# Two product sums in two PSUM banks per FFN unit, and two slot pools of six in a two-layer decoder trunk

## The chip, the cores and the metric

The kernel runs on one core of one Trainium2 chip. The metric is the device time of one execution in microseconds (us); the value for a kernel is the median over several executions. A profile is one more execution, recorded instruction by instruction. Engines: PE multiplies matrices (PEld is its weight load), DVE, ACT and POOL work on vectors, SP issues the transfers (DMA). PE writes its results to PSUM, eight banks of 512 numbers of 32 bits per partition; DVE and ACT read them there.

## The reference, cut to what matters

Two layers; each has two SwiGLU sub-layers (FFN), a token mixing and a per-layer embedding gate. All is computed in 32 bits, for 512 tokens of width 1024 and an FFN width of 2816.

```python
def swiglu(x, w_in, w_out):
    gate, up = jnp.split(x @ w_in, 2, axis=-1)
    return (jax.nn.silu(gate) * up) @ w_out

for l in range(DEPTH):                       # DEPTH = 2
    x = x + 0.5 * rms_norm(swiglu(rms_norm(x, ln_ffn1_pre[l]), w_ffn1_in[l], w_ffn1_out[l]), ln_ffn1_post[l])
    mix = token_mixing(rms_norm(x, ln_mix_pre[l]), ...)
    x = x + rms_norm(mix, ln_mix_post[l])
    x = x + 0.5 * rms_norm(swiglu(rms_norm(x, ln_ffn2_pre[l]), w_ffn2_in[l], w_ffn2_out[l]), ln_ffn2_post[l])
    gate = jax.nn.sigmoid(rms_norm(x, ln_ple_pre[l]) @ w_ple_gate[l])
    x = x + rms_norm(gate * (p[l] @ w_ple_proj[l]), ln_ple_post[l])
```

## The kernel before

**Precision.** A 32-bit operand is split into a high part (ACT, line 139) and a remainder, the low part (DVE, or POOL where a call says so, line 140). A product is three matmuls: high by high (L167), high by low (L168), low by high (L169); the third needs the low part of the weights.

**FFN-in** (function `ffn`) goes over 22 *units* m of 128 columns of gate and the 128 columns of up beside them. A unit is a 2 by 2 product of blocks done with seven products instead of eight; product n multiplies one combination of weight blocks with one combination of activation blocks (`right[n]`), in 4 slices of 3 matmuls of 256 columns, so 84 matmuls a unit. Products 1, 2, 3 and 5 have plain activations on the right (`xh`, `xl`; rows "p<-xh,w" and "p<-xl,w"), 4, 6 and 7 have sums of them (`tx`, rows "p<-tx,w"). On the left stand weights: `w12` (w1 for the first four units), `w75`, `w63` and `w4`; `ws` are the sums of blocks from which w75 and w63 are split (DVE lines 355, 357, 358). The split weights w12, w75 and w63 share NW = 3 buffers in the pool `wsp`, so the next unit's w12 is split once product 2 of this unit has read its own.

After the products DVE and ACT add the seven results up (lines 351 and 367 to 382) to `gate` (called a) and `up` (b), ACT applies Silu, DVE multiplies into `h`. A unit uses four of the eight PSUM banks: pa for products 1 and 2, pc for 6 and 3, pb for 7 and 5, pd for 4, each product in its own half of a bank.

At the **head** of FFN-in the four token blocks are turned (`turn`, PE transposes); for the last two of them the sums for tx are formed (lines 238 to 242), one of them (line 242) on POOL, which also splits three of the sums and the low parts of the first weights w1.

**FFN-out** (`ffn_out`) takes eleven blocks b of h in two column halves: seven as S blocks with seven-product sums, whose weights are loaded into `ws_r` (line 440) and read by PE as they are, four as plain P blocks, whose split h (`hq`) is kept for the second half. `us` holds evacuated sums at the end of a half.

**Slots.** Tiles of 8 KB (raw weights `wr`, `ws_r`, `hq`, h, tx, `xr`, `us`, split weights of some blocks) come from one pool of NS = 12; a load waits on SP's queue until a slot is free, and everything behind it in the queue waits as well.

**The order** on each engine is not the order of the code: the framework's scheduler sets it with its own timing model and fixes it at build time. Each engine then works strictly in that order.

Of the kernel before, what the change touches and what calls it, by code (L numbers as in the profile page):

```python
# [9 lines left out]
F32 = mybir.dt.float32  # L10
F32R = mybir.dt.float32r
# [6 lines left out]
S = 512  # L18
# [5 lines left out]
NS, NW = 12, 3  # L24
G = 4
# [47 lines left out]
class Trunk:  # L73
# [91 lines left out]
    def mm3(self, out, a, b, first, last):  # L165
        mm = self.nc.tensor.matmul
        mm(out, a[0], b[0], start=first, stop=False)  # L167
        mm(out, a[0], b[1], start=False, stop=False)  # L168
        mm(out, a[1], b[0], start=False, stop=last)  # L169
# [40 lines left out]
    def turn(self, t, xn, ffn):  # L210
# [31 lines left out]
        g_.tensor_tensor(t4, t4, t2, ALU.add)  # L242
# [19 lines left out]
    def out_proj(self, nb, part, blocks, gain, scale, after, tail):  # L262

        half0 = []
        for h in range(2):
# [13 lines left out]
            if h and tail == nb:  # L279
                raws = [q[:, j] for q in [self.slot([2, 1024], "wor") for _ in range(nb // 2)] for j in range(2)]  # L280
# [43 lines left out]
    def ffn(self, l, w, after):  # L324
# [15 lines left out]
        def product(n, q, out):  # L340
            for k in range(4):
                self.mm3(out, [a[:, k * 128:(k + 1) * 128] for a in q], [b[:, k] for b in right[n]], k == 0, k == 3)

        def left(m):
            r = self.ffn_raw[m] if m < G else self.ffn_load(l, w, [m])[0]
            return r, self.mm_tile("p12"), self.tmp.tile([128, S], F32, tag="tb0", name="gate", bufs=4)

        def gate(m, pa, a, q):
            product(1, self.cut(q, lo), pa[:, L])
            product(2, self.cut(q, hi), pa[:, H])  # L350
            a_.activation(a[:, (H, L)[m % 2]], pa[:, L], AF.Copy)

        def unit(m, r, pa, a):
# [11 lines left out]
            P, Q = (L, H) if m % 2 else (H, L)  # L365
            product(6, self.cut(sy, lo), pc[:, L])
            v_.tensor_tensor(a[:, Q], pc[:, L], a[:, P], ALU.add)
            product(7, self.cut(sx, lo), pb[:, P])
            product(5, self.cut(sx, hi), pb[:, Q])
            v_.tensor_tensor(b.rearrange("p (i t) -> p i t", i=2), pb.rearrange("p (i t) -> p i t", i=2),  # L370
                             a[:, None, Q].to_broadcast([128, 2, 256]), ALU.add)
            v_.tensor_tensor(a[:, P], pa[:, H], a[:, P], ALU.add)
            product(3, self.cut(sy, hi), pc[:, H])
            v_.tensor_tensor(a[:, Q], pc[:, H], b[:, Q], ALU.add)  # L374
            v_.tensor_tensor(b[:, Q], pb[:, Q], b[:, P], ALU.add)
            a_.activation(a, a, AF.Silu)  # L376
            product(4, u2, pd[:, L])
            v_.tensor_tensor(b[:, P], b[:, P], pd[:, L], ALU.subtract)
            if m % 4 == 0:
                hs.append(self.slot([8, 256], "h"))  # L380
# [18 lines left out]
    def ffn_out(self, hs, blocks, gain, scale, after):  # L399
# [50 lines left out]
        for h in range(2):  # L450
# [35 lines left out]
            us = self.slot([4, 512], "us")  # L486
# [1027 lines left out]
```

## Time and profile before

| | |
|---|---|
| median of 3 runs | 2292.49 us (2291.95 to 2295.7) |
| profiled execution | 2293.78 us, its span 2292.1 us |
| PE busy | 2154.4 us, 94% of the span |
| DVE busy | 1735.3 us, 76% |
| ACT busy | 1006.8 us, 44% |
| POOL busy | 330.7 us, 14% |
| FFN-in, first to last product | 17.44 to 289.99, 710.58 to 976.07, 1154.79 to 1426.45, 1845.73 to 2109.00 us |

The execution's own time is 1.7 us longer than its span, which runs from the first to the last instruction. A matmul's row lasts 0.28 us while the next starts 0.12 us after it: matmuls overlap, so a time per matmul is read from how many start in a stretch, not from a row's length. In rows of instructions, "[2.12 <-ACT w L139]" means that the engine stood idle for 2.12 us before this instruction until ACT's instruction of line 139 on tile w released it. PEclk is the clock that PE was granted, 1.00 being full speed.

### The profile page before, as it was taken

What the parts mean: (1) busy time and instruction counts of PE and PEld (TensorE: products, weight loads), DVE (VectorE), ACT (ScalarE), POOL (GpSimd) and SP (SyncE); (2) the same over time, 40 slices, a digit from 0 to 9 for tenths busy, and PEclk for the clock granted to TensorE, in tenths of its full rate; (3) what the DMA queues carried; (4) which work ended last, traced back from release to release, by engine and by line L of the source; (5) the groups of instructions that cost most, each with busy time, mean ns of one, the idle gap of its engine ahead of it and who ended that gap; (6) DMA issues with size and microseconds to landing.
All of it is one profiled execution on the core that took longest, in us unless ns stands there. A gap on an engine that the chain in (4) does not pass through costs nothing.

```text
span 2292.1 us, 39759 instructions
## 1 busy us (share of the span) xinstructions
PE 2154.4 (94%) x16256; PEld 1991.3 (87%) x16256; DVE 1735.3 (76%) x2886; ACT 1006.8 (44%) x1653; POOL 330.7 (14%) x424
## 2 busy tenths in 40 slices
PE   5999999999988999999979999999999989999998
PEld 5998999888767998999879899998887789899996
DVE  8988886555768888886688888775557698888774
ACT  4343433446545443433554344344464454344343
POOL 4000001132234000002330000111322330000111
PEclk9999999999999999999989999999999999999999
DMA  5222123322032222123322122243220322122232
GB/s 211 93 74 75 65 83 129 124 74 56 20 146 94 93 74 74 65 83 129 138 111 86 62 84 70 78 142 121 61 60 12 147 111 93 56 92 74 90 115 73
DMA packets 67495, 208.61 MB, mean 91 GB/s; under 512 B 15728, under 2 KB 16752, under 8 KB 67312
## 3 DMA queue, kind: packets, MB, share of 16 engines
q1 hardware_dynamic: 67312, 206.07, 25.5%
q8 instruction: 127, 2.08, 0.4%
q14 instruction: 56, 0.46, 0.1%
HBM read 199.23 MB, written 6.82 MB: 90 GB/s over the span
## 4 chain that ended last, share of the span: by engine, by line
PE 74%; DVE 12%; ACT 5%; DMA 3%; issue 3%; POOL 1%; SPq 0%; ACTq 0%; DVEq 0%; POOLq 0%
PE y L463 14%; PE p L169 12%; PE p L167 12%; PE p L168 12%; DVE w L140 2%; PE pkrv L169 1%; PE pkrv L168 1%; PE pkrv L167 1%; DVE xn L207 1%; PE y L169 1%; PE y L168 1%; PE y L167 1%; ACT w L139 1%; PE pgt L167 1%; PE pgt L168 1%
## 5 line engine op out<-in xcount | busy, mean ns | idle before, releaser
L167 PE MATMUL p<-xh,w 128*128 128x256 f32 x1408 | 415.9, 296 | 50.7 <-ACT w L139 46.3
L169 PE MATMUL p<-xh,w 128*128 128x256 f32 x1408 | 415.5, 295 | 9.8 <-POOL w L140 6.4
L168 PE MATMUL p<-xl,w 128*128 128x256 f32 x1408 | 411.6, 293 | 0.2 <-DVE xl L140 0.2
L167 PEld LDWEIGHTS p<-xh,w 128*128 128x128 f32 x1408 | 283.4, 202 | 57.0 <-ACT w L139 50.4
L167 PE MATMUL p<-tx,w 128*128 128x256 f32 x1056 | 301.3, 289 | 15.5 <-ACT tx L139 11.7
L168 PE MATMUL p<-tx,w 128*128 128x256 f32 x1056 | 296.8, 284 | 6.5 <-DVE tx L140 6.5
L169 PEld LDWEIGHTS p<-xh,w 128*128 128x128 f32 x1408 | 283.5, 201 | 15.1 <-DVE w L140 8.1
L169 PE MATMUL p<-tx,w 128*128 128x256 f32 x1056 | 293.3, 284 | 2.9 <-DVE w L140 2.9
L139 ACT ACTIVATE w<-ws 128x1024 fp32r<-128x1024 f32 x176 | 186.1, 1057 | 244.1 <-PE p L169 139.3
L168 PEld LDWEIGHTS p<-xl,w 128*128 128x128 f32 x1408 | 283.3, 201 | 0.9 <-DVE xl L140 0.8
L140 DVE TENSOR_TENSOR w<-ws,w 128x1024 fp32r<-128x1024 f32 x176 | 221.6, 1259 | 49.9 <-ACT w L139 46.9
L167 PEld LDWEIGHTS p<-tx,w 128*128 128x128 f32 x1056 | 202.8, 192 | 23.7 <-ACT tx L139 13.0
L168 PEld LDWEIGHTS p<-tx,w 128*128 128x128 f32 x1056 | 203.5, 193 | 7.6 <-DVE tx L140 7.6
L169 PEld LDWEIGHTS p<-tx,w 128*128 128x128 f32 x1056 | 199.7, 192 | 3.3 <-DVE w L140 3.2
L499 POOL TENSOR_TENSOR tb<-tb,ln_ffn_post 128x512 f32<-128x512 f32 x16 | 27.2, 1700 | 1192.6 <-ACT junk L196 1192.3
L463 PE MATMUL y<-wo,hq 128*128 128x256 f32 x1536 | 190.5, 282 | 0.0
L463 PEld LDWEIGHTS y<-wo,hq 128*128 128x128 f32 x1536 | 185.2, 190 | 0.4
L139 ACT ACTIVATE w<-wr 128x512 fp32r<-128x512 f32 (+1 forms) x176 | 144.2, 839 | 62.5 <-PE p L169 22.1
L463 PE MATMUL y<-ws_r,h 128*128 128x256 f32 x672 | 158.2, 379 | 0.0
L140 DVE TENSOR_TENSOR w<-wr,w 128x512 fp32r<-128x512 f32 (+1 forms) x161 | 152.4, 947 | 0.8 <-ACT w L139 0.7
L463 PEld LDWEIGHTS y<-ws_r,h 128*128 128x128 f32 x672 | 121.3, 190 | 13.4
L376 ACT ACTIVATE gate<-gate 128x512 f32<-128x512 f32 x88 | 54.9, 624 | 142.5 <-DVE gate L374 142.4
(426 smaller groups left out, 4745.7 us busy)
## 6 DMA issues: line engine op xcount, KB each, us to landing
wr<-in_w_ffn_in SPq DMA_DIRECT2D x176, 512.0 KB, 4.2
ws_r<-in_w_ffn_out SPq DMA_DIRECT2D x56, 512.0 KB, 3.7
wo_r<-in_w_ffn_out SPq DMA_DIRECT2D x32, 512.0 KB, 3.2
pkrv_r<-in_w_rw SPq DMA_DIRECT2D x16, 512.0 KB, 3.7
wpg_r<-in_w_ple_gate SPq DMA_DIRECT2D x16, 512.0 KB, 4.2
xd<-x SPq DMA_DIRECT2D x8, 512.0 KB, 3.1
x<-xd SPq DMA_DIRECT2D x8, 512.0 KB, 3.3
pq_r<-in_w_q SPq DMA_DIRECT2D x8, 512.0 KB, 3.5
```

The lines of the kernel that those rows point to most:

```text
L139: self.nc.scalar.activation(hi, src, AF.Copy)
L140: (eng or self.nc.vector).tensor_tensor(lo, src, hi.bitcast(F32), ALU.subtract)
L167: mm(out, a[0], b[0], start=first, stop=False)
L168: mm(out, a[0], b[1], start=False, stop=False)
L169: mm(out, a[1], b[0], start=False, stop=last)
L207: v_.scalar_tensor_tensor(xn[:, h], self.x[:, t, h], r, gain[:, h], ALU.mult, ALU.mult)
L376: a_.activation(a, a, AF.Silu)
L463: nc.tensor.matmul(banks[n][:, u], x, y, start=n not in seen, stop=last and i == len(todo) - 1, skip_group_check=True)
L499: (g_ if not h or QL[0] == "1" else v_).tensor_tensor(tb, tb, gain[:, h * 512:h * 512 + 512], ALU.mult)
```

## The change

- Two PSUM banks a unit instead of four. In bank pa, half L: product 1, read by ACT, then product 2 is added onto it by PE; half H: product 6. In bank pb, half L: product 5, read by ACT, then product 3 on top; half H: product 7, read by DVE, then product 4 on top. Only the first product of a bank sets the start flag.
- Order of the code within a unit: 1, 5, 2, 6, 7, 3, 4 (before 1, 2, 6, 7, 5, 3, 4). For the first four units `one` and `two` are called in a staggered way.
- Reading the sums: six DVE instructions (five of 256 columns, one of 512) instead of seven (five of 256, two of 512); four ACT instructions of 256 columns (two copies, two Silu) instead of one copy of 256 and one Silu of 512.
- The sum of line 242 moves from POOL to DVE, with the opposite sign, which turns product 4's sign.
- The twelve slots become two pools of six: "q" for wr (but not unit 3's), tx, hq, ws_r, wor and us, "h" for h, xr, unit 3's wr and the split weights.

```diff
-NS, NW = 12, 3
+NQ, NH, NW = 6, 6, 3
...
-        g_.tensor_tensor(t4, t4, t2, ALU.add)
+        v_.scalar_tensor_tensor(t4, t4, -1.0, t2, ALU.mult, ALU.subtract)
...
-        rs = [self.slot([2, 1024], "wr") for m in ms]
+        rs = [self.slot("h" if m == 3 else "q", [2, 1024], "wr") for m in ms]
...
-        def gate(m, pa, a, q):
-            product(1, self.cut(q, lo), pa[:, L])
-            product(2, self.cut(q, hi), pa[:, H])
-            a_.activation(a[:, (H, L)[m % 2]], pa[:, L], AF.Copy)
+        def one(m, pa, a, q):
+            product(1, self.cut(q, lo), pa[:, L], True, False)
+            a_.activation(a[:, places(m)[0]], pa[:, L], AF.Copy)
+        def two(m, pa, a, q):
+            product(2, self.cut(q, hi), pa[:, L], False, False)
...
-            pc, pb, pd = self.aux_tile("p63"), self.aux_tile("p75"), self.mm_tile("p4")
+            pb = self.aux_tile("p5374")
...
-            product(6, self.cut(sy, lo), pc[:, L])
-            v_.tensor_tensor(a[:, Q], pc[:, L], a[:, P], ALU.add)
-            product(7, self.cut(sx, lo), pb[:, P])
-            product(5, self.cut(sx, hi), pb[:, Q])
-            v_.tensor_tensor(b.rearrange("p (i t) -> p i t", i=2), pb.rearrange("p (i t) -> p i t", i=2),
-                             a[:, None, Q].to_broadcast([128, 2, 256]), ALU.add)
-            v_.tensor_tensor(a[:, P], pa[:, H], a[:, P], ALU.add)
-            product(3, self.cut(sy, hi), pc[:, H])
-            v_.tensor_tensor(a[:, Q], pc[:, H], b[:, Q], ALU.add)
-            v_.tensor_tensor(b[:, Q], pb[:, Q], b[:, P], ALU.add)
-            a_.activation(a, a, AF.Silu)
-            product(4, u2, pd[:, L])
-            v_.tensor_tensor(b[:, P], b[:, P], pd[:, L], ALU.subtract)
+            if q:
+                one(m, pa, a, q)
+            product(5, self.cut(sx, hi), pb[:, L], True, False)
+            a_.activation(b[:, P], pb[:, L], AF.Copy)
+            if q:
+                two(m, pa, a, q)
+            product(6, self.cut(sy, lo), pa[:, H], False, True)
+            v_.tensor_tensor(a[:, Q], pa[:, H], a[:, P], ALU.add)
+            product(7, self.cut(sx, lo), pb[:, H], False, False)
+            v_.tensor_tensor(b[:, Q], pb[:, H], a[:, Q], ALU.add)
+            a_.activation(a[:, P], pa[:, L], AF.Silu)
+            product(3, self.cut(sy, hi), pb[:, L], False, False)
+            v_.tensor_tensor(b[:, Q], b[:, Q], b[:, P], ALU.add)
+            product(4, u2, pb[:, H], False, True)
+            v_.tensor_tensor(b[:, P], pb[:, H], a[:, Q], ALU.add)
+            v_.tensor_tensor(a[:, Q], pb[:, L], a[:, Q], ALU.add)
+            a_.activation(a[:, Q], a[:, Q], AF.Silu)
...
-            r = self.slot([8, 256], "ws_r")
+            r = self.slot("q", [8, 256], "ws_r")
...
-            us = self.slot([4, 512], "us")
+            us = self.slot("q", [4, 512], "us")
```

In the changed kernel the lines of a unit are: 354 copy of product 1, 375 copy of product 5, 379 (reads 6), 381 (reads 7), 382 Silu of the half with 1 and 2, 384, 386 (reads 7 and 4), 387 (reads 5 and 3), 388 Silu of the other half, 392 into h; the sums ws are lines 362, 364 and 365.

**Where instructions now stand, ACT inside FFN-in.** Before, in the middle of the first FFN-in; p_ and w_ carry tile numbers, w_1775 and w_1778 are w75 and w63 of one unit, w_1863 is w12 of the next, L351 the copy of product 1, L376 the Silu.

```order
L139 ACTIVATE w_1775<-ws 128x1024 [waits PE_49]
L351 ACTIVATE gate<-p_1740 128x256 [waits PE_49]
L139 ACTIVATE w_1778<-ws 128x1024 [waits DVE_49,Activation_49]
L376 ACTIVATE gate<-gate 128x512 [waits DVE_49] x2
L139 ACTIVATE w_1863<-wr 128x1024 [waits DMAHW4_49,PE_49]
L139 ACTIVATE w_1902<-wr 128x512 [waits DMAHW5_49,PE_49,Activation_49]
```

The same place now, one whole unit; w_1730 is w12 of the next unit, L388 the late Silu of the unit before.

```order
L354 ACTIVATE gate<-p_1609 128x256 [waits PE_49]
L139 ACTIVATE w_1622<-ws 128x1024 [waits PE_49,Activation_49]
L139 ACTIVATE w_1625<-wr 128x512 [waits DMAHW1_49,PE_49,Activation_49]
L375 ACTIVATE up<-p_1629 128x256 [waits DVE_49,PE_49]
L139 ACTIVATE w_1730<-wr 128x1024 [waits DMAHW2_49,PE_49,Activation_49]
L388 ACTIVATE gate<-gate 128x256 [waits DVE_49]
L139 ACTIVATE w_1738<-ws 128x1024 [waits PE_49,Activation_49]
L382 ACTIVATE gate<-p_1609 128x256 [waits DVE_49,Activation_49]
```

The split of the next unit's w12 stood behind the Silu of this unit; now it stands ahead of a Silu, and that one belongs to the unit before. The pattern repeats every unit, before it repeated every four.

**DVE inside FFN-in.** Before, the rows up to the low part of the same w12 (w_1863).

```order
L367 TENSOR_TENSOR gate<-p_1785,gate 128x256 [waits PE_49]
L372 TENSOR_TENSOR gate<-p_1740,gate 128x256 [waits DVE_49]
L370 TENSOR_TENSOR up<-p_1786,gate 128x512 [waits PE_49]
L374 TENSOR_TENSOR gate<-p_1785,up 128x256 [waits DVE_49,PE_49]
L375 TENSOR_TENSOR up<-p_1786,up 128x256 [waits DVE_49]
L378 TENSOR_TENSOR up<-up,p_1787 128x256 [waits DVE_49]
L382 SCALAR_TENSOR_TENSOR h<-up,gate 128x512 [waits DVE_49,Activation_49,Pool_49]
L140 TENSOR_TENSOR w_1863<-wr,w_1863 128x1024 [waits DMAHW4_49,Activation_49]
```

Now, from one unit's sums to the next unit's; w_1500 and w_1503 are w75 and w63 of the next unit, w_1507 its w4, w_1611 the w12 after that.

```order
L381 TENSOR_TENSOR up<-p_1391,gate 128x256 [waits DVE_49,PE_49]
L384 TENSOR_TENSOR up<-up 128x256 [waits DVE_49]
L140 TENSOR_TENSOR w_1500<-ws,w_1500 128x1024 [waits Activation_49]
L362 TENSOR_TENSOR ws<-wr 128x1024 [waits DMAHW1_49,DMAHW0_49,DVE_49]
L140 TENSOR_TENSOR w_1503<-ws,w_1503 128x1024 [waits Activation_49]
L386 TENSOR_TENSOR up<-p_1391,gate 128x256 [waits PE_49]
L140 TENSOR_TENSOR w_1507<-wr,w_1506 128x512 [waits Activation_49]
L364 TENSOR_TENSOR ws<-ws,wr 128x512 [waits DVE_49]
L387 TENSOR_TENSOR gate<-p_1391,gate 128x256 [waits DVE_49]
L365 TENSOR_TENSOR ws<-ws,wr 128x512 [waits DVE_49]
L140 TENSOR_TENSOR w_1611<-wr,w_1611 128x1024 [waits Activation_49]
L379 TENSOR_TENSOR gate<-p_1490,gate 128x256 [waits PE_49]
```

The sums came in a block of seven; now they are spread between the splits, with the low part of w12 right ahead of the next unit's L379.

**POOL at the head of the first FFN.** Before, from the low parts of w1 of units 1 and 2 on:

```order
L140 TENSOR_TENSOR w_141<-wr,w_141 128x1024 [waits DMAHW2_49,Activation_49]
L140 TENSOR_TENSOR w_144<-wr,w_144 128x1024 [waits DMAHW3_49,Activation_49]
L140 TENSOR_TENSOR xl<-xr,xh 128x4x128 [waits Activation_49]
L242 TENSOR_TENSOR xr<-xr,tx 128x512 [waits DVE_49]
L140 TENSOR_TENSOR tx<-tx 128x4x128 [waits DVE_49,Activation_49]
L140 TENSOR_TENSOR w_147<-wr,w_147 128x1024 [waits DMAHW4_49,Activation_49]
```

Now:

```order
L140 TENSOR_TENSOR w_141<-wr,w_141 128x1024 [waits DMAHW7_49,Activation_49]
L140 TENSOR_TENSOR w_144<-wr,w_144 128x1024 [waits DMAHW0_49,Activation_49]
L140 TENSOR_TENSOR xl<-xr,xh 128x4x128 [waits Activation_49]
L140 TENSOR_TENSOR tx<-tx 128x4x128 [waits DVE_49,Activation_49]
L140 TENSOR_TENSOR xl<-xr,xh 128x4x128 [waits Activation_49]
L140 TENSOR_TENSOR w_147<-wr,w_147 128x1024 [waits DMAHW7_49,Activation_49]
```

Line 242 is gone from POOL, and the second xl has moved ahead of unit 3's w1.

More of the change, by code (lines that the diff above doesn't have):

```diff
@@ L163, in wblock, with mm3 @@
         return [self.cut(w, slice(i * c // 2, (i + 1) * c // 2)) for i in range(2)]
-    def mm3(self, out, a, b, first, last):
+    def mm3(self, out, a, b, first, last, shared=False):
         mm = self.nc.tensor.matmul
-        mm(out, a[0], b[0], start=first, stop=False)
-        mm(out, a[0], b[1], start=False, stop=False)
-        mm(out, a[1], b[0], start=False, stop=last)
+        mm(out, a[0], b[0], start=first, stop=False, skip_group_check=shared)
+        mm(out, a[0], b[1], start=False, stop=False, skip_group_check=shared)
+        mm(out, a[1], b[0], start=False, stop=last, skip_group_check=shared)
     def small(self, name, shape=(128, 1), dt=F32):
@@ L222, in turn @@
         if ffn and t == 0:
-            self.xr = self.slot([2, 8, 128], "xr")
+            self.xr = self.slot("h", [2, 8, 128], "xr")
         if ffn and t == 2:
-            self.tx = [self.slot([2, 4, 256], "tx", F32R) for _ in range(3)]
+            self.tx = [self.slot("q", [2, 4, 256], "tx", F32R) for _ in range(3)]
         if not ffn or t < 2:
@@ L338, in ffn, with product, unit @@
         lo, hi = slice(0, 512), slice(512, 1024)
-        def product(n, q, out):
+        def product(n, q, out, first, last):
             for k in range(4):
-                self.mm3(out, [a[:, k * 128:(k + 1) * 128] for a in q], [b[:, k] for b in right[n]], k == 0, k == 3)
+                self.mm3(out, [a[:, k * 128:(k + 1) * 128] for a in q], [b[:, k] for b in right[n]],
+                         first and k == 0, last and k == 3, True)
         def left(m):
             r = self.ffn_raw[m] if m < G else self.ffn_load(l, w, [m])[0]
-            return r, self.mm_tile("p12"), self.tmp.tile([128, S], F32, tag="tb0", name="gate", bufs=4)
-        def gate(m, pa, a, q):
-            product(1, self.cut(q, lo), pa[:, L])
-            product(2, self.cut(q, hi), pa[:, H])
-            a_.activation(a[:, (H, L)[m % 2]], pa[:, L], AF.Copy)
-        def unit(m, r, pa, a):
+            return r, self.mm_tile("p126"), self.tmp.tile([128, S], F32, tag="tb0", name="gate", bufs=4)
+        places = lambda m: (L, H) if m % 2 else (H, L)
+        def one(m, pa, a, q):
[3 more added lines that the diff above has]
+            product(2, self.cut(q, hi), pa[:, L], False, False)
+        def unit(m, r, pa, a, q):
             sx, sy = (self.wraw.tile([128, 1024], F32, tag="raw", name="ws") for _ in range(2))
@@ L385, in ffn @@
         first = [left(m) for m in range(G)]
-        for m, ((r, pa, a), q) in enumerate(zip(first, self.ffn_w1)):
+        for m in range(G + 1):
             if m in NFL:
                 self.flush(NFL[m])
-            gate(m, pa, a, q)
+            for f, i in ((one, m), (two, m - 1)):
+                if 0 <= i < G:
+                    f(i, *first[i][1:], self.ffn_w1[i])
         self.flush()
@@ L392, in ffn @@
             r, pa, a = first[m] if m < G else left(m)
-            if m >= G:
-                gate(m, pa, a, self.wsplit(r[:, 0], "w12"))
-            unit(m, r, pa, a)
+            unit(m, r, pa, a, self.wsplit(r[:, 0], "w12") if m >= G else None)
         wo = self.ins[f"w_ffn{w}_out"]
```

14 lines of the change are left out of this document (7 added, 7 removed).

## The prediction

> **What bounds the kernel now.** First I read the page, then PE's busy time in chosen stretches, then the instructions around one of its idle times.
>
> ```profile
> span 2292.1 us, 39759 instructions
> PE 5999999999988999999979999999999989999998
> PEclk9999999999999999999989999999999999999999
> ```
>
> PE is the engine to follow: it fills nearly every slice. But the slices hide what happens inside, so here are stretches (length, then PE, PEld, DVE, ACT, POOL busy with instruction counts, granted clock, DMA):
>
> ```profile
> core 0: us, PE busy (x) PEld busy (x) DVE busy (x) ACT busy (x) POOL busy (x), PEclk, DMA share, GB/s
> 186.00:222.00 36.00, 36.00 (x303) 35.80 (x303) 30.62 (x46) 14.59 (x20) 0.00 (x0) 1.00 0.32 118
> 90.36:135.03 44.67, 42.29 (x337) 41.66 (x337) 38.65 (x58) 17.92 (x25) 0.00 (x0) 0.96 0.20 72
> 135.03:179.71 44.68, 42.30 (x337) 41.67 (x337) 38.09 (x57) 18.19 (x25) 0.00 (x0) 0.96 0.20 72
> 179.71:224.75 45.04, 42.31 (x337) 41.49 (x337) 38.82 (x58) 18.19 (x25) 0.00 (x0) 0.96 0.25 94
> 225.20:228.60 3.40, 3.38 (x15) 3.09 (x15) 3.40 (x5) 1.07 (x2) 0.00 (x0) 0.50 0.00 0
> 300.00:400.00 100.00, 100.00 (x733) 96.45 (x733) 71.87 (x106) 37.67 (x48) 9.03 (x8) 1.00 0.31 106
> 710.58:733.25 22.67, 15.54 (x114) 13.84 (x114) 22.56 (x23) 14.78 (x27) 16.05 (x12) 0.94 0.52 185
> 45.35:289.99 244.64, 230.12 (x1791) 225.84 (x1792) 213.59 (x344) 99.26 (x133) 1.85 (x1) 0.95 0.21 76
> 733.25:976.07 242.82, 229.01 (x1792) 224.09 (x1793) 210.08 (x312) 98.74 (x128) 1.08 (x1) 0.96 0.21 77
> 1183.58:1426.45 242.87, 229.11 (x1792) 224.42 (x1793) 206.03 (x308) 98.54 (x128) 1.09 (x1) 0.96 0.22 77
> 1867.31:2109.00 241.69, 228.14 (x1792) 223.57 (x1793) 210.90 (x312) 99.38 (x130) 2.77 (x2) 0.96 0.22 78
> ```
>
> Undisturbed, 303 matmuls take 36.00 us, 0.119 each: a unit of 84 takes 9.98 us. Yet FFN-in goes in rounds of four units (337 matmuls) that take 44.67 to 45.04 us, against 4 x 9.98 = 39.9. Each round loses 4.75 to 5.1 us, on average 4.86. Why is in the instructions at a round's end, PE, ACT and DVE:
>
> ```profile
> 222.34 0.28 PE L169 MATMUL p<-xh,w 128*128 128x256 f32 x1
> 222.66 0.42 DVE L374 TENSOR_TENSOR gate<-p,up 128x256 f32<-128x256 f32 x1 [0.73 <-PE p L169]
> 223.12 0.63 ACT L376 ACTIVATE gate<-gate 128x512 f32<-128x512 f32 x1 [5.49 <-DVE gate L374]
> 223.66 1.56 ACT L139 ACTIVATE w<-wr 128x1024 fp32r<-128x1024 f32 x2
> 224.75 0.39 PE L167 MATMUL p<-xh,w 128*128 128x256 f32 x1 [2.12 <-ACT w L139]
> ```
>
> Product 3 ends; DVE sums (L374); only then can ACT's Silu run, which ACT had been waiting on for 5.49 us; behind it in ACT's order stands the split of the next unit's w12, and PE's next instruction needs that. PE stands for 2.12 us. Then comes a second payment: from 225.20 the clock is 0.50 for 3.4 us (15 matmuls in 3.40), some 1.7 us lost. 2.3 between starts, 1.7, and small waits make the 4.86. In FFN-out (300 to 400) PE has no idle time and full clock for 100 us, so load alone does not pull the clock down.
>
> The four FFN-in bodies (last four rows) take 241.7 to 244.6 us for about 1791 matmuls at the same clock of 0.95 to 0.96, so I count the first one's four rounds for each: 16 rounds, 16 x 4.86 = 78 us.
>
> **The change, part by part.**
>
> Durations inside a round (DVE, then ACT; the number after the comma is ns of one):
>
> ```profile
> L140 DVE TENSOR_TENSOR w<-ws,w 128x1024 fp32r<-128x1024 f32 x8 | 9.8, 1224 | 3.1 <-ACT w L139 2.9
> L355 DVE TENSOR_TENSOR ws<-wr 128x1024 f32<-128x1024 f32 x4 | 4.9, 1216 | 0.0
> L357 DVE TENSOR_TENSOR ws<-ws,wr 128x512 f32<-128x512 f32 x4 | 2.7, 683 | 0.0
> L370 DVE TENSOR_TENSOR up<-p,gate 128x512 f32<-128x512 f32 x4 | 2.7, 681 | 0.0
> L374 DVE TENSOR_TENSOR gate<-p,up 128x256 f32<-128x256 f32 x4 | 1.7, 421 | 0.7 <-PE p L169 0.7
> L382 DVE SCALAR_TENSOR_TENSOR h<-up,gate 128x512 f32<-128x512 f32 x5 | 3.4, 687 | 0.7 <-DVE up L378 0.5
> L139 ACT ACTIVATE w<-ws 128x1024 fp32r<-128x1024 f32 x8 | 8.5, 1057 | 10.2 <-PE p L169 6.2 <-DVE ws L355 2.3 <-issue 1.7
> L376 ACT ACTIVATE gate<-gate 128x512 f32<-128x512 f32 x4 | 2.5, 623 | 7.1 <-DVE gate L374 7.1
> L351 ACT ACTIVATE gate<-p 128x256 f32<-128x256 f32 x4 | 1.5, 380 | 7.3 <-PE p L169 7.3
> ```
>
> *Fewer sums.* L370 goes: 0.68 us of DVE per unit, 60 us over 88 units. ACT gets three instructions more and the Silu of 512 less: a Silu of 256 from PSUM lies between 0.38 (L351) and 0.62 (L376), I take 0.38, so 4 x 0.38 for 1.0, +0.5 us a unit or 45 us. Neither counts as time: DVE (38.8 of 45 us) and ACT (18.2) both have room beside PE.
>
> *The order.* Now w12's split stands ahead of a Silu whose sum (L387) DVE did a unit earlier, so the chain above is gone. What is late next? I walk one unit m, T from its product 5. Twelve matmuls are 1.43 us; PE: 5 and 2 until 2.85, 6 until 4.28, 7 until 5.70, the next unit's 1 until 7.13, 3 until 8.55, 4 until 9.98. A result is there 0.16 after the next start (0.28 less 0.12). w12 of m+1: buffer free after product 2, 3.01; ACT 1.06, 4.07; DVE 1.22, 5.29; product 1 needs it in its third matmul, 5.94. DVE then L379, L392, L381 (0.42, 0.69, 0.42): 6.82, and product 3, which may not start before L381 has read the bank, is due at 7.13: 0.3 left. L384: 7.24. w75 of m+1: free after 7, ACT 5.86 to 6.92, DVE 7.24 to 8.46, needed at 11. L362: 9.68. w63: free after 3, ACT 8.71 to 9.77, DVE until 10.99, needed at 13.1. L386, w4, L364, L387, L365 (0.42, 0.68, 0.68, 0.42, 0.68): 13.87, and the next w12 is ready for DVE at 9.98 + 4.07 = 14.05. The loop closes within 9.98 us, with 0.2 to 0.3 us to spare: PE is the bound, barely. So the 16 rounds gain their 78 us.
>
> *Shared banks.* A product now waits for the reader of the other half of its bank: 7 for the copy of 5, 3 for L381; and 2 for the copy of 1. Before, product 3 already waited for L367 on the other half:
>
> ```profile
> L167 PE MATMUL p<-xh,w 128*128 128x256 f32 x1408 | 415.9, 296 | 50.7 <-ACT w L139 46.3 <-DVE gate L367 2.8 <-ACT xh L139 1.6
> ```
>
> That wait cost 2.8 us in all. Three such waits give 8 us; at worst each read is exposed whole, (0.38 + 0.38 + 0.42) x 88 = 104 us, at best nothing. At least one other product stands between write and rewrite, so I take the near row: +8. [...]
>
> *Heads.* Before the bodies lie 22 to 29 us each in which PE waits; the second head, with L242 on POOL and a DVE instruction of 32 columns that POOL's work stretches (shortest, median, longest in ns):
>
> ```profile
> 725.30 0.38 PE L169 MATMUL p<-xh,w 128*128 128x256 f32 x1 [2.71 <-POOL w L140]
> 729.38 0.38 PE L167 MATMUL p<-tx,w 128*128 128x256 f32 x1 [1.19 <-ACT tx L139]
> 733.25 0.58 PE L168 MATMUL p<-tx,w 128*128 128x256 f32 x1 [2.21 <-DVE tx L140]
> L242 POOL TENSOR_TENSOR xr<-xr,tx x8: 1271/1300/2337, 26.7 to 1864.4; 128x512 f32<-128x512 f32 x8
> L1251 DVE TENSOR_SCALAR rope<-rope x3: 170/175/2423, 19.0 to 78.3; 128x32 f32<-128x32 f32 x3
> ```
>
> L242 leaves POOL's chain (2 x 1.30 a head) and costs DVE 2 x 0.69; and product 5 of unit 0, which needs no tx, now comes before 6 and 7: 1.43 us of work in a stretch of waiting. Against it, only three w buffers: product 2 of three units now comes after unit 3's w1. Bounds: 10 us lost to 7.1 gained (22.67 less 15.54) a head. I take 2 gained, the POOL and PE shares less the later w1: -8.
>
> *Tails.* Each round stretch ends in one longer stall where DVE also prepares FFN-out; that extra work stays, so I leave it: 0, bounds -20 (all four go with their clock) to +10.
>
> *Slots.* In FFN-in tx holds three of the six q slots; wr turns in the other three.
>
> ```profile
> wr<-in_w_ffn_in SPq DMA_DIRECT2D x176, 512.0 KB, 4.2
> ws_r<-in_w_ffn_out SPq DMA_DIRECT2D x56, 512.0 KB, 3.7
> L442 DVE TENSOR_TENSOR ws_r<-ws_r 128x512 f32<-128x512 f32 x9 | 6.2, 686 | 3.7 <-DMA ws_r<-in_w_ffn_out 3.7
> L444 DVE TENSOR_TENSOR ws_r<-ws_r 128x256 f32<-128x256 f32 x10 | 4.8, 493 | 0.0
> ```
>
> wr's slot is free after w4 of its unit (T = 2) and its next content is first read at T = 8.5 of the unit after: about 16 us for 2 x 4.2. Free. In FFN-out's second half four hq leave two slots for ws_r, and us holds one of them while the halves change, so the second load on SP's queue waits for the last sums; all loads behind it wait too. Landing 3.7 and preparation 0.69 + 0.42 + 0.49 face about 4 us of the first block: I take 1 us a half change, +4, bounds 0 and 15 (all of the 3.7 open). The gate stage shares six h slots: +2, by the same bounds.
>
> Sum: -78 + 8 - 8 + 4 + 2 = -72. The profiled execution took 2293.8 us, so 2221.8; the median is 1.3 lower: **2220 us**.
>
> **Rivals.**
>
> *The chain of 0.3 us breaks* (0.18). DVE meets work out of step, and PE waits before product 3 in every unit. At 0.5 us each, 64 units of the rounds give 32 us back: 2252. For: the narrow margin, and DVE at 86% of a round. Against: rows overlap, the walk used whole rows (a round's DVE rows add to 43.5 us, DVE was busy 38.8).
>
> *The gap is only moved* (0.06). ACT still meets a Silu or copy that waits for DVE just ahead of a split: 2.1 us a round and the clock drop stay, 2292. For: ACT is in order and L382 waits for L379. Against: in the walk L379 ends at 5.7, before ACT reaches L382.
>
> *The clock drops are not the gaps' doing* (0.04). They recur about every 44 us, so they could belong to sustained load; then 16 x 1.7 = 27 us stay: 2247. Against it stands the row of 100 us at 1.00. [...]
>
> *Slower: the q pool starves FFN-out* (0.06). If us or a late hq leaves one slot for ws_r through the second halves, each of the 28 blocks there waits for its own load: 28 x 3.7 = 104, 2324. It turns the sign from 2.6 us a block on. For: SP's queue stops at the first load without a slot. Against: each block's slot is free once its plain matmuls and its split are through, well before its sums end.
>
> **How the numbers follow.** The forecast has 0.62, from 2195 (tails go, heads gain) to 2235 (heads gain nothing, banks double). The rivals have 0.18, 0.06, 0.04, 0.06; 0.04 is left over for heads that lose. For 8 in 10 the range runs from 2195 to 2256, over the broken chain and the clock. Faster by over 0.2% (4.6 us, about what can be told from no change): forecast, broken chain, clock, part of the rest, 0.89; within it 0.04 (the moved gap); slower 0.07.
>
> **What the profile after would show.** PE's stretches in FFN-in: 337 matmuls in 40 to 40.5 us and PEclk at 1.00 in place of 0.96. No ACT Silu ahead of a PE wait. DVE busy near 34 of 40. If the chain breaks, p L167 waits on DVE up L381 by tens of us. If the pool starves, waits of PE on ws_r appear after each FFN-in. I would be wrong most of all if DVE's rows grow longer when it, ACT and PE share banks.

## The result, and the profile after

| | before | changed |
|---|---|---|
| median, 4 runs each | 2294.1 us | 2193.1 us (2189.5 to 2196.5) |
| ratio | | 0.9558, 95% interval 0.9537 to 0.9579 |
| span of the profiled execution | 2292.1 us | 2190.5 us |
| PE busy | 94% | 97% |
| half clock up to PE's last matmul | 116.0 us (34 windows of 3.413 us) | 44.4 us (13) |

The median before is that of the three runs given above and one more. The change saves 4.4%, 101 us. Forecast were 72 us and a range that ended at 2195 us on its fast side: the direction and the mechanism of the rounds held, and the gain came out 29 us larger, just beyond that range. Three rows of the page of the changed kernel:

```profile
span 2190.5 us, 39798 instructions
PE   6999999999989999999989999999999989999998
PEclk8999999999999999999999999999999999999999
```

A stretch of about four units in the second FFN-in, first of the changed kernel, and then (for the first experiment) of the old kernel with nothing but the two pools; columns as in the stretches of before:

```profile
775.25:815.31 40.06, 40.06 (x339) 40.06 (x338) 35.91 (x53) 20.64 (x32) 0.00 (x0) 1.00 0.29 106
```

```profile
775.25:815.31 40.06, 40.06 (x339) 40.06 (x338) 37.23 (x58) 18.38 (x25) 0.00 (x0) 1.00 0.32 115
```

339 matmuls in 40.06 us at full clock, where before 337 took 44.7. The round of four units is gone; a unit repeats every 10.01 us, as the two splits of w12 in ACT's rows of the changed kernel show (ACT first, then DVE):

```profile
805.30 1.06 ACT L139 ACTIVATE w<-wr 128x1024 fp32r<-128x1024 f32 x1 [0.39 <-PE p L169]
806.26 0.40 ACT L388 ACTIVATE gate<-gate 128x256 f32<-128x256 f32 x1
...
815.31 1.06 ACT L139 ACTIVATE w<-wr 128x1024 fp32r<-128x1024 f32 x1 [0.38 <-PE p L169]
...
806.39 1.23 DVE L140 TENSOR_TENSOR w<-wr,w 128x1024 fp32r<-128x1024 f32 x1 [0.60 <-ACT w L139]
807.53 0.42 DVE L379 TENSOR_TENSOR gate<-p,gate 128x256 f32<-128x256 f32 x1
807.87 0.68 DVE L392 SCALAR_TENSOR_TENSOR h<-up,gate 128x512 f32<-128x512 f32 x1
808.47 0.42 DVE L381 TENSOR_TENSOR up<-p,gate 128x256 f32<-128x256 f32 x1
```

The split of w12 waits for PE alone, and the Silu behind it is ready when its turn comes. DVE even idles 0.60 us ahead of its part. Some of PE's waits, of the whole program, in total, times and longest; before, then changed (tb are sums that DVE prepares after FFN-out, pkv and pgt products of the token mixing and of the embedding gate):

```profile
PE p L167 <- ACT w L139: 49.6, 32, 3.1
PE pkv L167 <- DVE tb L497: 3.2, 2, 2.3
```

```profile
PE p L167 <- ACT w L139: 7.1, 5, 3.9
PE p L167 <- ACT gate L354: 4.0, 4, 2.0
PE p L167 <- ACT up L375: 2.8, 1, 2.8
PE pgt L167 <- DVE tb L507: 2.3, 2, 1.2
PE p L167 <- DVE up L381: 1.6, 4, 0.5
PE pkv L167 <- DVE tb L507: 0.4, 1, 0.4
```

To put the 101.6 us in their places, each FFN-in is cut by PE's matmuls: the head up to the first of unit 4 (matmul 336 in the order they start), 16 units of rounds (to matmul 1680), and the tail with the rest of FFN-in and the first 48 matmuls of FFN-out, which stand among them. From each piece 0.1188 us a matmul (36.00/303) is taken away, so what is left is loss; the 12 to 16 transposes of a head are not counted as matmuls, so their time is part of its loss. "Rest" is all other time; the matmuls' own 4 x 1896 x 0.1188 = 901 us complete the span. Sums over the four FFN-in, us, from the traces:

| profiled kernel | heads | rounds | tails | rest | span | median of runs |
|---|---|---|---|---|---|---|
| before | 67.8 | 77.3 | 30.8 | 1215.2 | 2292.1 | 2294.1 |
| changed | 69.7 | 4.7 | 3.2 | 1211.9 | 2190.5 | 2193.1 |
| old, two pools | 67.8 | 0.6 | 9.6 | 1203.9 | 2182.8 | 2186.1 |
| changed, one pool | 64.8 | 116.4 | 35.7 | 1221.0 | 2338.8 | 2338.9 |
| old, two pools, 20 stops forced | 69.1 | 81.2 | 17.5 | 1211.2 | 2279.9 | 2279.7 |
| old, two pools, product 5 first | 57.8 | 0.9 | 9.3 | 1211.0 | 2179.9 | 2180.4 |

### The profile page after: what moved, and what is told of

Same layout as the page of the kernel before. It is cut to its first block, busy times and chain, and to the rows that moved or that the text cites. A ratio compares the mean times of both kernels' runs of the same rounds, so it can differ in the third digit from the quotient of the medians.

```text
span 2190.5 us, 39798 instructions
## 1 busy us (share of the span) xinstructions
PE 2114.6 (97%) x16256; PEld 1962.5 (90%) x16256; DVE 1674.6 (76%) x2806; ACT 1058.5 (48%) x1829; POOL 307.8 (14%) x416
## 3 DMA queue, kind: packets, MB, share of 16 engines
q1 hardware_dynamic: 67312, 206.07, 26.8%
## 4 chain that ended last, share of the span: by engine, by line
PE 80%; DVE 9%; ACT 5%; issue 2%; DMA 2%; POOL 1%; SPq 0%; DVEq 0%; POOLq 0%; ACTq 0%
PE y L473 17%; PE p L167 13%; PE p L169 12%; PE p L168 12%; PE pkrv L169 1%; PE pkrv L168 1%; PE pkrv L167 1%; DVE xn L207 1%; PE y L168 1%; PE y L167 1%; PE y L169 1%; DVE w L140 1%; PE pgt L167 1%; PE pgt L169 1%; PE pgt L168 1%
## 5 line engine op out<-in xcount | busy, mean ns | idle before, releaser
L167 PE MATMUL p<-xh,w 128*128 128x256 f32 x1408 | 404.6, 291 | 14.4 <-ACT w L139 7.1
L168 PE MATMUL p<-xl,w 128*128 128x256 f32 x1408 | 400.3, 287 | 0.4 <-DVE xl L140 0.4
L169 PE MATMUL p<-xh,w 128*128 128x256 f32 x1408 | 394.4, 288 | 4.2 <-DVE w L140 2.8
L167 PEld LDWEIGHTS p<-xh,w 128*128 128x128 f32 x1408 | 274.5, 195 | 20.2 <-ACT w L139 8.8
L168 PEld LDWEIGHTS p<-xl,w 128*128 128x128 f32 x1408 | 275.1, 195 | 1.3 <-DVE xl L140 1.3
L169 PEld LDWEIGHTS p<-xh,w 128*128 128x128 f32 x1408 | 270.3, 195 | 6.2 <-DVE w L140 4.1
L140 DVE TENSOR_TENSOR w<-ws,w 128x1024 fp32r<-128x1024 f32 x176 | 216.1, 1228 | 45.5 <-ACT w L139 44.9
L167 PEld LDWEIGHTS p<-tx,w 128*128 128x128 f32 x1056 | 200.2, 190 | 3.6 <-ACT up L375 3.0
L169 PEld LDWEIGHTS p<-tx,w 128*128 128x128 f32 x1056 | 199.2, 189 | 3.0 <-DVE w L140 2.9
L168 PEld LDWEIGHTS p<-tx,w 128*128 128x128 f32 x1056 | 199.8, 189 | 0.0
L139 ACT ACTIVATE w<-wr 128x512 fp32r<-128x512 f32 (+1 forms) x176 | 148.8, 846 | 61.2 <-PE p L169 34.8
L139 ACT ACTIVATE wb<-ws_r 128x1024 fp32r<-128x1024 f32 x56 | 59.1, 1055 | 126.6 <-DVE ws_r L453 59.6
```

What stands on the lines that cost most here:

```text
L139: self.nc.scalar.activation(hi, src, AF.Copy)
L140: (eng or self.nc.vector).tensor_tensor(lo, src, hi.bitcast(F32), ALU.subtract)
L167: mm(out, a[0], b[0], start=first, stop=False, skip_group_check=shared)
L168: mm(out, a[0], b[1], start=False, stop=False, skip_group_check=shared)
L169: mm(out, a[1], b[0], start=False, stop=last, skip_group_check=shared)
```

## Experiments: which part of the change

**The pools alone, and everything but the pools.** The old kernel with two pools (the lines are those of the change's diff that name a slot; of the function `unit` only the slot call for h is touched):

```diff
-NS, NW = 12, 3
+NQ, NH, NW = 6, 6, 3
-        rs = [self.slot([2, 1024], "wr") for m in ms]
+        rs = [self.slot("h" if m == 3 else "q", [2, 1024], "wr") for m in ms]
...
```

> The kernel before, with nothing changed but the two pools of six in place of the one of twelve; four PSUM banks a unit, the old order of products and the whole Silu stay. Theory A (the pools alone set where the next unit's w12 split stands on ACT; the PSUM sums only free DVE): the 20 stops of about 2.1 us with their clock drops go, and 2294 falls to 2195 to 2225; it stays above 2193 because DVE keeps the instruction of 0.68 us a unit and has 9.7 us of work in a unit of 9.98. Rival B (the sums in PSUM and the new order of products make the difference, the pools nothing): 2285 to 2296, stops as before.

And the changed kernel with one pool again:

```diff
-NQ, NH, NW = 6, 6, 3
+NS, NW = 12, 3
-        return self.slots.tile([128] + list(shape), dt, tag=tag, name=name, bufs={"q": NQ, "h": NH}[tag])
+        return self.slots.tile([128] + list(shape), dt, tag="s", name=name, bufs=NS)
```

> The changed kernel with one pool of twelve again; PSUM sums, order of products and halves of Silu stay changed. Theory A (the pools): five stops of PE return in each FFN-in, one every four units, each about 2 us with a clock drop behind it; 20 x (2.1 + 1.7) = 76 us, so 2255 to 2290. Rival B (PSUM sums and order): 2190 to 2205, no stops.

Measured: 2186.1 us with the pools alone (ratio 0.9539, 0.9521 to 0.9558), 2338.9 with everything but the pools (1.0195, 1.0175 to 1.0215). Theory A stands, though both its ranges were missed (2195 to 2225 and 2255 to 2290): the pools gain more than it said, and without them the rest of the change costs time. All of the gain is the pools'. The sums in PSUM, the new order of products and the halved Silu gain nothing: without the pools the kernel is 45 us slower than before, and with them 2193.1 stands against 2186.1 without (the intervals of the two ratios overlap, so that this 0.3% is not sure). The row of the pools alone above says why the freed DVE time was not needed: four units need 37.23 us of DVE in 40.06, and that fits.

The changed kernel with one pool, PE's waits:

```profile
PE p L167 <- ACT w L139: 53.8, 25, 3.3
PE p L169 <- DVE w L140: 16.2, 24, 0.9
PE p L167 <- DVE up L381: 11.7, 23, 0.7
```

Its rounds lose 7.3 us each (116.4/16) where before they lost 4.8: the stop for w12 is back, and with it come more waits for low parts of weights (5.9 us in the program before) and for the shared bank (L381), where the old banks cost 2.8 us (L367). At 11 of the 16 stops in the rounds two windows of half clock follow instead of one.

In the fixed order on ACT, old and new, the cause can be counted: with one pool the split of w12 stands behind the Silu of the unit just before it at units 5, 9, 13, 17 and 21 of each FFN-in, in the old kernel and in the changed one alike. With two pools it does so nowhere, except where the runs below force it.

## Experiments: is it the order, or are slots late?

**The split written earlier.** One pool, old sums; the next unit's load and split moved ahead in the code:

```diff
             if m >= G:
-                gate(m, pa, a, self.wsplit(r[:, 0], "w12"))
+                gate(m, pa, a, nq)
+            if G <= m + 1 < NM:
+                nr = self.ffn_load(l, w, [m + 1])[0]
+                nq = self.wsplit(nr[:, 0], "w12")
             unit(m, r, pa, a)
```

> The kernel before with one pool of twelve and all sums as they were; only the load and the split of the next unit's w12 are written one unit earlier in the code, so that on ACT the split always stands ahead of the Silu of the unit before it. Theory A1 (the stop is the order on ACT alone; the loads have long landed): the stops go as with two pools, 2195 to 2230. Rival A2 (with one pool the slots really come free late on the chip, the order only mirrors it): PE waits for ACT's split, and that for its load; 2265 or more.

Measured: 2281.9 us (0.9936, 0.9913 to 0.9959), rounds 90.7, tails 6.7. That is A2's number, but not its mechanism; ACT, then PE, of this kernel:

```profile
818.15 0.63 ACT L375 ACTIVATE gate<-gate 128x512 f32<-128x512 f32 x1 [6.95 <-DVE gate L373]
818.68 1.04 ACT L139 ACTIVATE w<-wr 128x1024 fp32r<-128x1024 f32 x1
...
819.77 0.39 PE L167 MATMUL p<-xh,w 128*128 128x256 f32 x1 [2.12 <-ACT w L139]
```

ACT waits for DVE and not for a load. The order did move, but not as it was meant to: the splits for units 5, 9, 13, 17 and 21 now stand well ahead of that Silu, and those for units 6, 10, 14 and 18 stand right behind the Silu of two units before, so 16 stops are left. So this run doesn't tell A1 from A2. But it has no such stop in the tails, and they lose 6.7 us in place of 30.8.

**The order forced.** Two pools, old sums, and after every fourth unit the split made to depend on the Silu:

```diff
             a_.activation(a, a, AF.Silu)
+            self.ffn_one = None
+            if m and m % 4 == 0:
+                self.ffn_one = self.small("one")
+                a_.activation(self.ffn_one, a[:, 0:1], AF.Copy, scale=0.0, bias=1.0)
...
-            gate(m, pa, a, self.wsplit(r[:, 0], "w12"))
+            gate(m, pa, a, self.wsplit(r[:, 0], "w12", scale=self.ffn_one))
```

> The kernel before with the two pools (2186.1 us) in which, after every fourth unit, the split of the next unit's w12 is made to wait for the Silu of the unit before (its scale is a column of ones that ACT derives from the Silu's output); five such places in each FFN-in, where the kernel before stopped. Nothing else changes. If the order on ACT is what costs (the loads being early): 20 stops of 2.1 to 2.4 us, each with a window of half clock behind it (1.7), 2186 + 20 x (3.8 to 4.9) = 2262 to 2285. If the late freeing of slots in one pool was the cost and the order only its picture: 2186 to 2196.

Measured: 2279.7 us, 93.6 above the pools alone; ACT, then PE, at a forced place:

```profile
860.60 0.63 ACT L380 ACTIVATE gate<-gate 128x512 f32<-128x512 f32 x1 [1.37 <-DVE gate L378]
861.26 0.20 ACT L384 ACTIVATE one<-gate 128x1 f32<-128x1 f32 x1
861.49 1.15 ACT L147 ACTIVATE w<-wr,one 128x1024 fp32r<-128x1024 f32 x1
...
862.69 0.39 PE L171 MATMUL p<-xh,w 128*128 128x256 f32 x1 [2.59 <-ACT w L147]
863.95 0.58 PE L173 MATMUL p<-xh,w 128*128 128x256 f32 x1 [0.76 <-DVE w L148]
```

The rounds lose 81.2 us, 5.1 each, where before's lost 77.3, 4.8 each. The slots are the same as in the fast kernel; the order differs, and 20 ACT instructions of some 0.2 us (L384) that carry the dependency: the order on ACT is the cost, and the pools matter because they change it. In the kernel before, too, no load was late at a stop. The loads of wr from 180 to 226 us, around its stop at 222.6 (time of the issue, shortest, median and longest, and first and last start; then time to landing):

```profile
L316 SPq DMA_DIRECT2D wr<-in_w_ffn_in x8: 328/380/434, 185.5 to 210.7; - x8
DMA to landing us min/median/max: 3.2/3.7/4.2
```

The last one had landed by 214.9, and the split began at 223.66. At all 20 stops every load of wr issued by then had landed at least 2.1 us before the split, which followed on ACT without a pause. What in one pool of twelve makes the scheduler go by fours is not shown; its own timing model leaves no trace.

## Experiments: the half clock

The prediction priced a stop with 1.7 us of half clock behind it. Four windows of 3.41 us of the kernel before, around its stop at 222.6 to 224.75:

```profile
218.31:221.72 3.41, 3.41 (x30) 3.40 (x29) 1.60 (x4) 0.00 (x0) 0.00 (x0) 1.00 0.00 0
221.72:225.13 3.41, 1.28 (x10) 1.00 (x8) 2.50 (x6) 2.01 (x3) 0.00 (x0) 1.00 0.00 0
225.13:228.55 3.42, 3.40 (x16) 3.04 (x15) 3.42 (x5) 1.14 (x2) 0.00 (x0) 0.51 0.00 0
228.55:231.96 3.41, 3.17 (x26) 2.96 (x26) 3.20 (x4) 1.86 (x3) 0.00 (x0) 0.99 0.02 5
```

PE is busy for 1.28 us of the second window, and exactly the third runs at half clock. To test that it is the idle share, the forced splits were made in pieces, so that the stops shrink:

```diff
-            self.nc.scalar.activation(w[:, 0], src, AF.Copy, scale=scale)
-            self.nc.vector.tensor_tensor(w[:, 1], src, w[:, 0].bitcast(F32), ALU.subtract)
+            for c in (slice(0, 256), slice(256, 512), slice(512, 1024)):
+                self.nc.scalar.activation(w[:, 0, c], src[:, c], AF.Copy, scale=scale)
+                self.nc.vector.tensor_tensor(w[:, 1, c], src[:, c], w[:, 0, c].bitcast(F32), ALU.subtract)
```

> The kernel with the 20 forced stops (2279.7 us), in which those splits of w12 are made in pieces of 256, 256 and 512 columns, so that PE starts again after the first. There PE now stands 1.92 us, starts two matmuls and stands 1.04 us for the low part; ACT's first piece takes some 0.38 in place of 1.06 us and DVE's 0.42 in place of 1.22, so a stop loses about 1.2 to 1.4 us less, 2279.7 - 20 x 1.3 = 2254. Theory G (the half clock follows when PE has been idle for more than about half of one window of 3.41 us): the idle time falls from 2.7 to about 1.4 us, most windows of half clock behind the stops go too, another 20 x 1.7: 2216 to 2230. Rival H (any stop brings the window, or sustained load does): they stay, 2250 to 2258.

Measured: 2259.0 us, which is just beyond H's end and far from G's. But the idle time did not fall as the expectation had it: with the new order nine of the 16 stops in the rounds still part two starts by 2.23 us. Where they did shrink (1.28 and 0.5 us, or 1.56 and 0.5) no half clock follows; 14 of the 16 had it behind them with the whole split, 5 have it now. Two of the 2.23 stops, each with its window and the next:

```profile
1244.09:1247.51 3.42, 2.47 (x21) 2.26 (x20) 2.50 (x5) 1.09 (x2) 0.00 (x0) 1.00 0.00 0
1247.51:1250.92 3.41, 2.31 (x17) 2.10 (x18) 2.94 (x6) 3.35 (x7) 0.00 (x0) 1.00 0.00 0
1288.47:1291.88 3.41, 1.37 (x10) 0.96 (x8) 3.02 (x7) 1.98 (x6) 0.00 (x0) 1.00 0.00 0
1291.88:1295.29 3.41, 3.38 (x16) 3.39 (x17) 3.05 (x4) 2.27 (x3) 0.00 (x0) 0.50 0.38 117
```

The first lies across the edge of two windows, PE is busy for 2.47 and 2.31 us in them, and the clock stays; the second lies inside one, 1.37 busy, and the clock halves. So G is right about the cause, as the count over all runs in the last section bears out, and was wrong about the size, because the stops shrank less than expected; H falls.

## Experiment: the tail

The failed step of the prediction was tested by itself: the forced order at one place only, the split for the last unit of each FFN-in.

```diff
-            if m and m % 4 == 0:
+            if m == 20:
```

> The kernel before with the two pools (2186.1 us), in which only the last of the five places is forced: the split of the last unit's w12 waits for the Silu of the unit before it; once in each FFN-in. Theory E (the loss at the end of FFN-in was a fifth stop of the same kind, left out of the forecast's count): each tail loses 2 us by the stop and 1.7 more where a window of half clock follows, 2194 to 2203; the kernel before lost 5.3 us more per tail than the one with two pools. Rival F (as forecast: the tail's loss comes from DVE's extra preparation of FFN-out, whatever the order): 2184 to 2189.

Measured: 2209.3 us (0.9626, 0.9613 to 0.9639), 23 above the pools alone. The tails lose 27.2 us in place of 9.6, nearly the 30.8 of before; the rounds stay at 0.5. So the loss there hangs on that one split and not on FFN-out's preparation alone: F falls. Over all 14 kernels the tails follow that one place: where the last split of w12 stands behind the Silu of the unit just before it (before, one pool, the three forced kernels) they lose 17.5 to 35.7 us, in the nine others 2.7 to 11.7. The size, beyond E's range too, is not a clean price of the stop. PE's waits at one such tail:

```profile
907.49 0.38 PE L171 MATMUL p<-xh,w 128*128 128x256 f32 x1 [1.43 <-DVE gate L371]
911.77 0.39 PE L171 MATMUL p<-xh,w 128*128 128x256 f32 x1 [0.32 <-ACT w L147]
914.32 2.06 PE L471 MATMUL y<-ws_r,h 128*128 128x256 f32 x4 [2.04 <-DMA ws_r<-in_w_ffn_out]
```

The scheduler filled the forced place with other products, and the stop came out as a wait for a bank's sum and one for FFN-out's load; the rest grew by 8.4 us too. With all 20 stops forced, the fifth ones cost 7.9 us together (17.5 against 9.6), and no half clock follows them there.

## Experiments: the heads, and a better version

**Line 242 and the stagger**, in five kernels; each undoes or does one of the two. The changed kernel with the sum on POOL:

```diff
-        v_.scalar_tensor_tensor(t4, t4, -1.0, t2, ALU.mult, ALU.subtract)
+        g_.tensor_tensor(t4, t4, t2, ALU.add)
...
```

> The changed kernel with the sum of line 242 on POOL again (the sign of product 4 is turned in w4's split, same number of instructions). Theory C (on DVE the sum stands in the first head's longest chain, which lost 8 us up to unit 4): the first head gets 3 to 8 us back, the others move by 1 or less, 2185 to 2191. Rival D (POOL's chain sets the heads, as forecast): each head loses about 2 us, 2199 to 2203. If neither engine is the bound there: within 2 us of 2193.

The opposite, on the old kernel with two pools:

> The kernel before with the two pools, and the sum of line 242 on DVE. In the changed kernel the same move was worth 5.8 us (2198.9 on POOL, 2193.1 on DVE). If that gain belongs to the heads: 2180 to 2184. If it was the accident of one order: 2185 to 2190.

The stagger alone, on the old kernel with two pools:

```diff
+        for m in range(G + 1):
...
+            for f, i in ((one, m), (two, m - 1)):
+                if 0 <= i < G:
+                    f(i, *first[i][1:], self.ffn_w1[i])
```

> The kernel before with the two pools, and products 1 and 2 of the first four units staggered as in the changed kernel (all products 1 early, each 2 one unit later). The changed kernel reached unit 4 7.5 us later in the first head and 5.0 us earlier in the third; if the stagger makes both, the sum is 2186 to 2190; if it makes only the third head's gain, 2181; if PSUM accumulation made it, no change, 2185 to 2187.

The changed kernel without the stagger, and the same with line 242 on POOL:

> The changed kernel without the stagger: products 1 and 2 of each of the first four units stand together in the code again; two pools, PSUM sums and the order 5, 2, 6, 7, 3, 4 stay. With the old sums the stagger cost 13.8 us (2199.9 against 2186.1). If the stagger is the whole loss of the changed kernel against the pools alone (7 us): 2180 to 2187. If the PSUM sums lose by themselves (a unit of 10.01 us where the pools alone reach 9.98, and the copies that product 2 waits for): 2190 to 2200.

> The same without the stagger, and with the sum of line 242 on POOL. On DVE that sum was worth 5.8 us with the stagger and cost 4.2 us with the old sums. If its worth belongs to the stagger (DVE then has time where POOL is late): 2176 to 2184, below the run beside it. If it belongs to the PSUM sums: 2186 to 2196, above it by 4 to 6.

| kernel | median | ratio, interval | heads | rounds | tails | rest |
|---|---|---|---|---|---|---|
| changed, 242 on POOL | 2198.9 | 0.9589, 0.9575 to 0.9604 | 67.3 | 4.7 | 2.7 | 1222.6 |
| old, two pools, 242 on DVE | 2190.3 | 0.9550, 0.9537 to 0.9563 | 70.6 | 1.4 | 9.3 | 1205.2 |
| old, two pools, stagger | 2199.9 | 0.9587, 0.9573 to 0.9600 | 61.5 | 14.1 | 11.7 | 1210.4 |
| changed, no stagger | 2195.2 | 0.9579, 0.9564 to 0.9594 | 69.7 | 4.7 | 3.0 | 1219.3 |
| the same, 242 on POOL | 2197.2 | 0.9586, 0.9573 to 0.9599 | 68.0 | 4.7 | 2.7 | 1221.3 |

Most expectations missed. Line 242 does little in the heads either way (67.3 against 69.7, 70.6 against 67.8), less than the rest moves: C falls, and so does D, whose number came out (2198.9) while the heads lost nothing. The stagger alone gains 6.3 us in the heads and loses 13.5 in the rounds, where PE now waits for ACT's copy of product 1 (L350: 21.1 us in 31 waits over the program). Taken out of the changed kernel it changes nothing in FFN-in: PE's products stand in the same order there and the heads are 28.7, 13.2, 14.9 and 12.9 us with and without, so the scheduler staggers these products by itself. Its 2195.2 us lie in the range expected of sums that lose by themselves, and the first head fits that (28.7 us, with the pools alone 21.2). The 2 us between 2195.2 and 2193.1 are within the two intervals; the profiled executions of these two differ in the rest, where three windows of half clock (two from 1050.5 and one at 1726.3) appear in the one and not in the other. Apart from the pools, no experiment meant to touch the rest, and it lies anywhere between 1203.9 and 1222.6 us; 7 us between two kernels can be just that.

**Product 5 ahead of 6 and 7**, which need the sums tx, on the old kernel with two pools:

```diff
+            product(5, self.cut(sx, hi), pb[:, Q])
             product(6, self.cut(sy, lo), pc[:, L])
...
-            product(5, self.cut(sx, hi), pb[:, Q])
```

> The kernel before with the two pools, and product 5, which needs no sums of activations, written ahead of products 6 and 7. If the heads wait for those sums (waits of up to 5.8 us there): 12 matmuls, 1.4 us, fill each head, 4 x 1 to 2 us, 2178 to 2183. If the order in the head is bound elsewhere, or the new order upsets the rounds (DVE has 9.7 us of work in 9.98): 2184 to 2200.

Measured: 2180.4 us (0.9506, 0.9493 to 0.9519), 0.6% below the changed kernel and the fastest here; the two intervals do not touch. Each head gains 1.3 to 3.3 us, 10.0 in all, of which the rest takes 7 back in the profiled executions. PE's waits for tx with the two pools alone:

```profile
PE p L167 <- ACT tx L139: 11.0, 5, 5.5
PE p L168 <- DVE tx L140: 7.4, 4, 2.7
PE p L167 <- ACT xh L139: 1.6, 3, 0.7
```

and with product 5 first the one is gone and the other is short, but a wait for xh, the plain activations, takes part of their place:

```profile
PE p L167 <- ACT xh L139: 15.0, 6, 5.1
PE p L168 <- DVE tx L140: 1.2, 1, 1.2
```

## What the prediction had right, and where it failed

- *Rounds, -78 and +8 for shared banks.* Measured 77.3 to 4.7, -72.6 against -70. The chain named (product 3, sum, Silu, split, PE) is the cause, as the forced order shows, and the walk's period was right, 10.01 us against 9.98. The +8 came out by luck: PE's waits for readers of its banks (L354, L375, L381) add up to 8.4 us in the program, but every one of them stands in a head, and in the 64 units of the rounds the profile lists none. So the row of 2.8 us still came nearer than the 104. A wait on the other half of a bank did occur (at 61.40, in the first head, a product with tx waited 2.75 us for the copy of product 5, L375), but in the rounds such waits cost nothing. What the prediction credited to the change as a whole, though, belongs to the pools; it never asked which part of the change moved the split.
- *Tails, 0.* This step failed. "That extra work stays, so I leave it" took the last stall for FFN-out's preparation. It was a fifth stop of the same chain, with a split of FFN-out's `hq` in it, so the sum counted 16 stops where there are 20 (four more at its 4.86 us would have been 19 us); the kernel before, ACT and then PE:

```profile
267.99 0.63 ACT L376 ACTIVATE gate<-gate 128x512 f32<-128x512 f32 x1 [5.49 <-DVE gate L374]
268.53 1.04 ACT L139 ACTIVATE hq<-h 128x1024 fp32r<-128x1024 f32 x1
269.48 1.56 ACT L139 ACTIVATE w<-wr 128x1024 fp32r<-128x1024 f32 x2
270.57 0.58 PE L167 MATMUL p<-xh,w 128*128 128x256 f32 x1 [3.07 <-ACT w L139]
```

  The same wait of 5.49 us on L374 as in the quoted round, and 3.07 us for PE with 3.4 to 6.8 us of half clock in each tail. The tails went from 30.8 to 3.2 us: -27.6, beyond the bound of -20; 21.2 of it come with the pools alone, 6.4 with the rest of the change. That the split's place makes the loss is shown above; how the 27.6 divide between the stop and what follows it stays open. The span fell by 29.6 us more than forecast; the other three terms missed by -2.6, +9.9 and -9.3 and nearly cancel.
- *Heads, -8.* Measured +1.9. The first lost 7.9 us and the third gained 5.4; the others gained or lost under 1. About 351 matmuls from the first product on, the changed kernel and then the one before, first and third head:

```profile
14.51:82.94 68.43, 55.71 (x351) 52.20 (x352) 62.84 (x114) 31.82 (x54) 18.97 (x11) 0.83 0.26 96
1107.81:1162.62 54.81, 47.05 (x353) 44.69 (x354) 49.76 (x69) 31.21 (x55) 14.62 (x13) 0.94 0.23 78
```

```profile
17.44:78.16 60.72, 48.00 (x351) 46.00 (x350) 58.62 (x93) 27.12 (x41) 21.23 (x11) 0.92 0.36 136
1154.79:1215.00 60.21, 48.73 (x352) 46.78 (x353) 53.25 (x70) 28.59 (x46) 20.87 (x15) 0.86 0.29 106
```

  In the first head PE is idle as long as before (12.7 us) and busy 7.7 us longer, at a lower clock. In the third it is idle 3.7 us less and busy 1.7 us less. That the clock makes the first head longer is not shown: with line 242 on POOL that head has 10.2 us of half clock, as before's has, and still loses 26.8 us against 20.8. The kernels with the new sums lose 24.6 to 28.7 us there, those with the old sums 18.7 to 21.8; which part of the new sums and their order does it stays open. Nor does half clock in a head always cost: the changed kernel without the stagger has 13.7 us of it in the third head, the changed one 6.8, and both take 54.8 us for it. The step that product 5 fills the wait was right where it stood alone (10 us with the two pools).
- *Rest, +4 and +2.* Measured -3.3. The two stretches from FFN-out through the embedding gate took 2.0 and 2.5 us more (PE pgt waits 1.2 for DVE's tb), where +2 in all was forecast. Against that the first product starts 2.9 us earlier (14.51 against 17.44), and the two stretches from FFN-out through the token mixing are 2.6 and 2.2 us shorter: the first mixing no longer waits 2.3 us for DVE (pkv, above), and the window of half clock behind that went too. No load of ws_r starved in the changed kernel.
- *Rivals.* The chain of 0.3 us held: PE waited for L381 four times, 1.6 us in all. The gap was not moved either: PE's wait for ACT's w fell from 49.6 to 7.1 us. In these runs the clock drops are the gaps' doing: none of 8449 windows in which PE was idle for under 35% was followed by one (last section). In the traces of both kernels all edges of the half clock, but for the end of the last stretch, lie on a grid of 3.413 us (28 stretches before, 7 in the changed kernel), and the window from 221.72 to 225.13 of before, which PE spent 62% idle (1.28 us busy of 3.41), was followed by one at 0.51.

## What to carry to other kernels

When a stall recurs, count its places in the fixed order of the engine in front of it, to the end of the stage: the last one may be dressed as something else. A pool of buffers that tiles of different lifetime share can cost through the order that the scheduler makes of it, with every transfer in time; try the split of the pools alone before the arithmetic that comes with it. And price a stop by where it falls: of the two stops of 2.23 us shown above, the one inside a window of 3.413 us had a window at 0.50 behind it, some 1.7 us more by the estimate below, and the one across two windows had none.

## What the runs showed of the hardware

How the granted clock went with PE's idle time was counted. Over the 14 profiled executions, 8728 windows of 3.413 us at full clock were compared with the clock of the next: with PE idle for under 35%, none of 8449 was followed by half clock; between 35 and 60%, 62 of 170; above 60%, all 109 (the kernel before and the changed one alone: none of 1200, 10 of 26, all 23). The lowest share with a drop was 0.38, the highest without one 0.54 (idle time as the trace's modelled ends of matmuls give it). Of 281 windows at half clock none with more than 19% idle time was followed by full clock. The stop of 2.12 us at 222.6 of the kernel before lay inside one window; the next ran at 0.51, and 16 matmuls started in its 3.42 us where 30 had started in the window ahead of the stop. That is some 1.7 us more for this stop, an estimate: half of 3.413. Half clock fell from 116.0 to 44.4 us; this is at most 36 us of lost time, an estimate that takes PE as the bound in all of it, and so up to a third of the whole gain.
